# Products 512 columns wide, a token-major gated feed-forward and weights loaded in pairs: a two-layer encoder trunk on one core

## The chip, the core and the metric

The kernel runs on one core of a Trainium2 chip. TensorE (PE) multiplies, with its weight loads shown as an engine of their own (PEld); VectorE (DVE), ScalarE (ACT) and GpSimd (POOL) work element by element; SyncE (SP) issues nearly all the DMAs. PE reads SBUF and writes PSUM, whose banks here hold 128 x 512 floats. The metric is the device time of one execution in microseconds (us), as the median of several runs; lower is better.

## The reference

The input x is 256 tokens of 1024 features, in float32. Two layers, each of them:

```
x += 1/2 * (silu(n(x) @ w1) * (n(x) @ w3)) @ w2        # feed-forward 1, 1024 -> 2816 -> 1024
proj = n(x) @ w_in                                      # 1024 -> 3840 columns
A = retention(4 heads), B = HGRN2 (4 heads), C = RG-LRU # chunks of 64 tokens, from proj
x += concat(A, B, C) @ w_out
x += cross_attention(n(x), n(mem))                      # 4 heads, 256 memory tokens: wq, wkv, wo
x += 1/2 * (silu(n(x) @ w1) * (n(x) @ w3)) @ w2        # feed-forward 2
```

`n` is an RMSNorm with a gain; a last norm closes the trunk. All weights are float32, about 214 MB, and each is read once.

## The kernel before

**Products in three parts.** Every float32 operand of a large product is split into two float32r parts, hi + lo, and the product is the sum of three: hi\*hi, hi\*lo and lo\*hi (`mm3`, lines L175 to L178; the two PE lines in the profile are L169 and L171). Each of the three is one TensorE instruction with a stationary operand of 128 x 128 and a moving one of 128 x 256.

**Two ways round.** In `gemm_w` the weight piece is stationary and the 256 tokens stream, so that the result is feature-major (features on partitions). It makes w1, w3, w2, six of the fifteen 256-column pieces of w_in, the keys, w_out, wq and wo. In `gemm_x` the tokens are stationary and 256 weight columns stream, so that the result is token-major: nine pieces of w_in, the values, and the very last w2 (`final`).

**Weights.** `Weights` streams the weights in pieces of 512 rows x 256 columns (512 KB, 414 loads in all) through four raw buffers. `_split` makes the two parts: ACT copies to float32r (L82), DVE subtracts (L83). There are three buffers for the parts, so the split of a piece waits until PE is through with the piece three before it; `take` issues splits three ahead and loads five ahead.

**Feed-forward.** For every 256 of the 2816 columns, w1 and w3 give u and v for two 128-feature tiles. DVE multiplies by 1 / rms (L372, tile `R`, the factor in every row), ACT takes silu, DVE multiplies (L376), and `split` makes `g_hi` and `g_lo`. `residual` then multiplies by w2, adds to xT tile by tile (`add_tile`, L345) and makes the two parts of the next norm's input, `xn_hi` and `xn_lo`. `finish` makes `R` with a plain float32 product (L337).

**Mixers and attention.** `STEPS` sets the order in which the w_in pieces and the elementwise chains of HGRN2, retention and RG-LRU come. A scheduler then orders each engine's instructions; products that wait for nothing (the keys and the values of the cross-attention, `mem_h` and `mem_l`) fill the time in which the chains run on DVE and ACT. At the end of the chains the gated heads are transposed on PE (L544) into w_out's input, `mix_hi` and `mix_lo`. In the attention the scores of each head stand ahead of the value product of the head before.

Of the kernel before, what the change touches and what calls it, by code (L numbers as in the profile page):

```python
# [15 lines left out]
P = 128  # L16
D = 1024
# [9 lines left out]
SPLIT_AHEAD = 3  # L27
LOAD_AHEAD = 5
RAW_BUFS = 4
SPLIT_OFF = 100000  # L30
EVAC_OFF = 400
O_AHEAD = 1
KV_OFF = 100000
PART_BUFS = 3
E_BUFS = 1
# [15 lines left out]
SILU = "silu_and_others"  # silu, tanh, sin  # L51
# [4 lines left out]
class Weights:  # L56
    """Streams the packed pieces of the weights and splits them into two float32r parts."""

    def __init__(self, tc, pool, flat, pieces):
        self.tc, self.nc, self.pool = tc, tc.nc, pool  # L60
        self.flat, self.pieces = flat, pieces
        self.raw, self.parts = {}, {}
        self.n_load = self.n_split = self.n_take = self.off = 0

    def _load(self):
        i = self.n_load
        self.n_load += 1
        n = self.pieces[i].nk * CW
        t = self.pool.tile([P, 4 * CW], F32, name="w_raw", tag="w_raw", bufs=RAW_BUFS)
        self.nc.sync.dma_start(  # L70
            out=t[:, 0:n], in_=self.flat[self.off:self.off + P * n].rearrange("(p c) -> p c", p=P))
        self.off += P * n
        self.raw[i] = t.rearrange("p (k c) -> p k c", k=4)

    def _split(self):
        nc, i = self.nc, self.n_split
        self.n_split += 1
        nk = self.pieces[i].nk
        t = self.raw.pop(i)
        hi = self.pool.tile([P, 4, CW], F32R, name="w_hi", tag="w_hi", bufs=PART_BUFS)  # L80
        lo = self.pool.tile([P, 4, CW], F32R, name="w_lo", tag="w_lo", bufs=PART_BUFS)
        nc.scalar.copy(hi[:, 0:nk, :], t[:, 0:nk, :])  # L82
        nc.vector.tensor_tensor(  # L83
            out=lo[:, 0:nk, :], in0=t[:, 0:nk, :], in1=hi[:, 0:nk, :].bitcast(F32), op=ALU.subtract
        )
        self.parts[i] = (hi, lo)

    def take(self, key):
        i = self.n_take
        self.n_take += 1  # L90
        assert self.pieces[i].key == key, (self.pieces[i], key)
        with self.tc.high_priority(offset=SPLIT_OFF):
            while self.n_load < min(i + LOAD_AHEAD, len(self.pieces)):
                self._load()
            while self.n_split < min(i + SPLIT_AHEAD, len(self.pieces)):
                self._split()
        return (*self.parts.pop(i), self.pieces[i].nk)
# [5 lines left out]
IN_COLS = [1536, 1792, 2048, 2304] + [int(x) for x in STEPS if x.isdigit()]  # L103


# (column piece, first row tile) of xattn_wo: the first heads' rows of some columns fill the wait for the last heads
O_ORDER = [(c, 0) for c in range(O_AHEAD)] + [(c, 4) for c in range(O_AHEAD)]
O_ORDER += [(c, k0) for c in range(O_AHEAD, 4) for k0 in (0, 4)]

Piece = namedtuple("Piece", "key name l k0 nk c0")  # L110


def weight_pieces():
    """[nk * 128, 256] pieces of the weights in the order in which they are used"""
    out = []

    def gemm(key, name, l, nk, cs):
        for c in cs:
            for k0 in range(0, nk, 4):
                out.append(Piece(key, name, l, k0, min(4, nk - k0), c))  # L120

    for l in range(DEPTH):
        for f in ("ffn1", "ffn2"):
            if f == "ffn2":
                gemm("in", "w_in", l, KD, IN_COLS)
                gemm("kv", "xattn_wkv", l, KD, range(0, 2 * D, CW))
                gemm("out", "w_out", l, KD, range(0, D, CW))
                gemm("q", "xattn_wq", l, KD, range(0, D, CW))
                out += [Piece("o", "xattn_wo", l, k0, 4, c * CW) for c, k0 in O_ORDER]
            for c in range(0, FF, CW):  # L130
                gemm("w1", f + "_w1", l, KD, [c])
                gemm("w3", f + "_w3", l, KD, [c])
            gemm("w2", f + "_w2", l, KF, range(0, D, CW))
    # the first column's pieces in halves, for an early start
    return [out[0]._replace(nk=2, k0=k0) for k0 in range(0, KD, 2)] + out[2:]
# [9 lines left out]
def trunk(ctx: ExitStack, tc: tile.TileContext, a: dict, out: bass.AP, stop=None, dbg=None):  # L145
# [9 lines left out]
    class Bank:  # L155
        """A PSUM bank in which several sums may be open: only the first product clears the written bits"""
# [18 lines left out]
        def mm3(self, acc, lhs, rhs, begin, stop):  # L175
            (lh, ll), (rh, rl) = lhs, rhs
            self.mm(acc, lh, rh, begin, False)
            self.mm(acc, lh, rl, False, False)  # L178
            self.mm(acc, ll, rh, False, stop)

    class Act:
        """Activations that need a table: each table is loaded once for a run of them, in the order of the program"""
# [14 lines left out]
        def hold(self, i):  # L197
            """the next table waits for this instruction too"""
# [14 lines left out]
    W = Weights(tc, wp, a["weights"], weight_pieces())  # L213
# [37 lines left out]
    def split(hi, lo, src, scale=None):  # L251
        """hi + lo == src (* a column) with both parts in float32r"""
# [9 lines left out]
    def gemm_w(key, nk, x, accs):  # L262
        """acc += w[:, m]^T x for two column tiles m; accs = (bank, acc), x = (hi, lo) of [P, nk, S]"""
        xh, xl = x
        k0 = 0
        while k0 < nk:
            wh, wl, n = W.take(key)
            for m, (bank, acc) in enumerate(accs):
                for k in range(n):
                    sl = slice(m * P, (m + 1) * P)  # L270
                    bank.mm3(acc, (wh[:, k, sl], wl[:, k, sl]), (xh[:, k0 + k, :], xl[:, k0 + k, :]),
# [4 lines left out]
    def gemm_x(key, nk, x, accs, begin=True):  # L276
        """accs[t] = (bank, acc), acc += x[:, t]^T w for two token tiles t"""
        xh, xl = x
        k0 = 0
        while k0 < nk:  # L280
            wh, wl, n = W.take(key)
            for t, (bank, acc) in enumerate(accs):
                for k in range(n):
                    sl = slice(t * P, (t + 1) * P)
                    bank.mm3(acc, (xh[:, k0 + k, sl], xl[:, k0 + k, sl]), (wh[:, k, :], wl[:, k, :]),
                             begin and k0 + k == 0, k0 + k == nk - 1)
            k0 += n
            yield
# [5 lines left out]
    class Norm:  # L294
        """RMSNorm of the residual: x * g goes out in two float32r parts, the 1 / rms is applied after the product"""

        def __init__(self, l, name, mem=False):
            self.gains = col(l, name)
            if not mem:
                self.hi = keep.tile([P, KD, S], F32R, name="xn_hi", tag="xn_hi", bufs=1)  # L300
                self.lo = keep.tile([P, KD, S], F32R, name="xn_lo", tag="xn_lo", bufs=1)
            self.ssq = small.tile([P, S], F32, name="ssq", tag="ssq", bufs=2)

        def parts(self, j, xj):
            split(self.hi[:, j, :], self.lo[:, j, :], xj, self.gains[:, j:j + 1])

        def square_first(self, j, xj):
            """square() on GpSimd, for the start, when the other engines are wanted for the splits"""
            if j == 0:
                nc.gpsimd.tensor_tensor(out=self.ssq, in0=xj, in1=xj, op=ALU.mult)  # L310
            else:
                sq = small.tile([P, S], F32, name="sq", tag="sq", bufs=2)
# [3 lines left out]
        def square(self, j, xj):  # L316
            if j == 0:
                nc.scalar.square(self.ssq, xj)
            else:
                sq = small.tile([P, S], F32, name="sq", tag="sq", bufs=2)  # L320
# [3 lines left out]
        def finish(self, R=None):  # L324
            """1 / rms, rc in columns and R in every row"""
            pr = aux_bank()
            self.R = small.tile([P, S], F32, name="R", tag="R", bufs=2) if R is None else R
# [3 lines left out]
            rsqrt_col(self.rc, pr[:, 0:2], 2)  # L331
            dg = small.tile([P, 2, P], F32, name="r_diag", tag="r_diag", bufs=1)
# [7 lines left out]
        @property  # L340
        def x(self):
            return self.hi, self.lo

    def add_tile(j, acc, scale, nxt):
        nc.vector.scalar_tensor_tensor(out=xT[:, j, :], in0=acc, scalar=scale, in1=xT[:, j, :],  # L345
                                       op0=ALU.mult, op1=ALU.add)
# [3 lines left out]
    def residual(key, nk, x, scale, nxt):  # L350
        """xT += scale * (w^T x), and prepares the next norm tile by tile"""
        for c in range(0, KD, 2):
            banks = [mm_bank(2) for _ in range(2)]
            yield from gemm_w(key, nk, x, [(b, b[:, 0, :]) for b in banks])
            for m in range(2):
                add_tile(c + m, banks[m][:, 0, :], scale, nxt)
        nxt.finish()

# [1 line left out]
    def ffn(l, f, nrm, nxt, last=False, setup=None):  # L360
        with tc.tile_pool(name="ffn", bufs=2) as fp:
            gh = fp.tile([P, KF, S], F32R, name="g_hi", bufs=1)
            gl = fp.tile([P, KF, S], F32R, name="g_lo", bufs=1)
            if setup is not None:
                setup = setup(fp)
            for c in range(0, KF, 2):
                uv = [mm_bank(2) for _ in range(2)]
                for u, key in enumerate(("w1", "w3")):
                    run(gemm_w(key, KD, nrm.x, [(b, b[:, u, :]) for b in uv]))
                for m in range(2):  # L370
# [712 lines left out]
```

## Time and profile before

| | |
|---|---|
| median of 3 runs | 1274.72 us (1274.69 to 1274.8) |
| profiled execution, first to last instruction | 1272.7 us |
| PE busy | 1256.4 us, 99% |
| DVE, ACT busy | 877.4 us (69%), 682.3 us (54%) |
| DMA | 219.64 MB, mean 173 GB/s |

The runs lie 2.0 us above the span of the profiled execution, which is what lies around the first and the last instruction. Matmuls are pipelined and their ends are modelled, so PE's busy time says only that something was always under way; how fast it went is read from the distance between starts.

### The profile page before, as it was taken

What the parts mean: (1) busy time and instruction counts of PE and PEld (TensorE: products, weight loads), DVE (VectorE), ACT (ScalarE), POOL (GpSimd) and SP (SyncE); (2) the same over time, 40 slices, a digit from 0 to 9 for tenths busy, and PEclk for the clock granted to TensorE, in tenths of its full rate; (3) what the DMA queues carried; (4) which work ended last, traced back from release to release, by engine and by line L of the source; (5) the groups of instructions that cost most, each with busy time, mean ns of one, the idle gap of its engine ahead of it and who ended that gap; (6) DMA issues with size and microseconds to landing.
All of it is one profiled execution on the core that took longest, in us unless ns stands there. A gap on an engine that the chain in (4) does not pass through costs nothing.

```text
span 1272.7 us, 26847 instructions
## 1 busy us (share of the span) xinstructions
PE 1256.4 (99%) x11134; PEld 1249.8 (98%) x11134; DVE 877.4 (69%) x1456; ACT 682.3 (54%) x1149; POOL 42.6 (3%) x68
## 2 busy tenths in 40 slices
PE   7999999999999999999999999999999999999997
PEld 7999999999999999999999999999999999999997
DVE  7886656988776676665586665578877767666653
ACT  4554445656765654444464444465577656444543
POOL 5000000000100000000000000000001000000000
PEclk9999999999999999999999999999999999999999
DMA  8756566555465465665566665654545645666563
GB/s 269 211 175 184 174 185 190 157 149 150 117 182 165 115 184 183 183 182 182 183 209 202 181 184 179 187 177 154 159 121 149 183 133 165 183 183 182 168 181 100
DMA packets 61946, 219.64 MB, mean 173 GB/s; under 512 B 6912, under 2 KB 7168, under 8 KB 61568
## 3 DMA queue, kind: packets, MB, share of 16 engines
q1 hardware_dynamic: 60768, 213.55, 56.2%
q0 software_dynamic: 768, 3.86, 0.8%
q8 instruction: 87, 1.43, 0.5%
q10 hardware_dynamic: 288, 0.52, 0.1%
q14 instruction: 35, 0.29, 0.1%
HBM read 216.85 MB, written 1.05 MB: 171 GB/s over the span
## 4 chain that ended last, share of the span: by engine, by line
PE 83%; issue 15%; DVE 1%; DMA 0%; ACT 0%; POOLq 0%; POOL 0%; SPq 0%; ACTq 0%
PE mm L171 75%; PE aux L171 2%; PE aux L663 1%; PE mm L169 1%; PE aux L661 0%; PE aux L169 0%; DVE xn_lo L258 0%; PE aux L656 0%; PE aux L800 0%; PE aux L731 0%; PE aux L788 0%; DMA xT<-in_x_t_dram 0%; PE aux L337 0%; PE aux L901 0%; DVE w_lo L83 0%
## 5 line engine op out<-in xcount | busy, mean ns | idle before, releaser
L83 DVE TENSOR_TENSOR w_lo<-w_raw,w_hi 128x1024 fp32r<-128x1024 f32 (+1 forms) x414 | 498.9, 1206 | 281.3 <-ACT w_hi L82 278.6
L82 ACT CAST w_hi<-w_raw 128x1024 fp32r<-128x1024 f32 (+1 forms) x414 | 425.5, 1029 | 491.8 <-PE mm L171 371.3
L171 PE MATMUL mm<-xn_hi,w_lo 128*128 128x256 f32 x1728 | 487.6, 285 | 2.1 <-DVE w_lo L83 2.1
L171 PE MATMUL mm<-xn_lo,w_hi 128*128 128x256 f32 x1728 | 488.0, 284 | 0.0
L171 PE MATMUL mm<-xn_hi,w_hi 128*128 128x256 f32 x1620 | 457.8, 284 | 6.2 <-ACT w_hi L82 6.2
L171 PEld LDWEIGHTS mm<-xn_hi,w_lo 128*128 128x128 f32 x1728 | 330.4, 192 | 3.4 <-DVE w_lo L83 3.0
L171 PEld LDWEIGHTS mm<-xn_lo,w_hi 128*128 128x128 f32 x1728 | 331.6, 192 | 0.1
L171 PEld LDWEIGHTS mm<-xn_hi,w_hi 128*128 128x128 f32 x1620 | 311.1, 192 | 6.3 <-ACT w_hi L82 6.2
L171 PE MATMUL mm<-g_hi,w_hi 128*128 128x256 f32 x528 | 147.1, 280 | 0.0
L171 PE MATMUL mm<-g_lo,w_hi 128*128 128x256 f32 x528 | 146.1, 278 | 0.0
L171 PE MATMUL mm<-g_hi,w_lo 128*128 128x256 f32 x528 | 145.2, 281 | 0.0
L171 PEld LDWEIGHTS mm<-g_lo,w_hi 128*128 128x128 f32 x528 | 99.3, 188 | 0.0
L171 PEld LDWEIGHTS mm<-g_hi,w_hi 128*128 128x128 f32 x528 | 99.3, 188 | 0.0
L171 PEld LDWEIGHTS mm<-g_hi,w_lo 128*128 128x128 f32 x528 | 97.9, 188 | 0.0
L171 PE MATMUL mm<-w_hi,xn_lo 128*128 128x256 f32 x288 | 81.8, 284 | 0.0
L171 PE MATMUL mm<-w_lo,xn_hi 128*128 128x256 f32 x288 | 81.8, 284 | 0.0
L171 PE MATMUL mm<-w_hi,xn_hi 128*128 128x256 f32 x270 | 76.4, 285 | 0.0
L372 DVE TENSOR_TENSOR f_t<-mm,R 128x512 f32<-128x512 f32 x88 | 60.1, 687 | 3.6 <-ACT R L338 1.4
L171 PEld LDWEIGHTS mm<-w_hi,xn_lo 128*128 128x128 f32 x288 | 55.2, 192 | 0.1
L171 PEld LDWEIGHTS mm<-w_lo,xn_hi 128*128 128x128 f32 x288 | 55.2, 192 | 0.1
L171 PEld LDWEIGHTS mm<-w_hi,xn_hi 128*128 128x128 f32 x270 | 51.5, 192 | 0.0
L171 PE MATMUL mm<-w_lo,g_hi 128*128 128x256 f32 x176 | 49.3, 281 | 0.0
(269 smaller groups left out, 1955.7 us busy)
## 6 DMA issues: line engine op xcount, KB each, us to landing
w_raw<-in_weights_dram SPq DMA_DIRECT2D x394, 512.0 KB, 3.7
w_raw<-in_weights_dram SPq DMA_DIRECT2D x20, 256.0 KB, 2.7
m_t<-in_mem_t_dram POOLq DMA_DIRECT2D x2, 1024.0 KB, 7.9
xT<-in_x_t_dram SPq DMA_DIRECT2D x4, 256.0 KB, 4.9
cst<-in_c_cst_dram POOLq DMA_DIRECT2D x1, 696.0 KB, 6.4
gw<-in_gates_w_dram POOLq DMA_DIRECT2D x2, 256.0 KB, 8.5
fg<-in_final_norm_g_dram POOLq DMA_DIRECT2D x1, 512.0 KB, 5.9
out_dram<-y SPq DMA_DIRECT2D x2, 256.0 KB, 2.6
```

Source lines behind the costliest of these rows:

```text
L82: nc.scalar.copy(hi[:, 0:nk, :], t[:, 0:nk, :])
L83: nc.vector.tensor_tensor(out=lo[:, 0:nk, :], in0=t[:, 0:nk, :], in1=hi[:, 0:nk, :].bitcast(F32), op=ALU.subtract)
L169: nc.tensor.matmul(acc, lhsT, rhs, start=False, stop=stop, skip_group_check=True)
L171: i = nc.tensor.matmul(acc, lhsT, rhs, start=begin, stop=stop, skip_group_check=True)
L372: nc.vector.tensor_tensor(out=t, in0=uv[m].ap, in1=nrm.R[:, None, :].to_broadcast([P, 2, S]), op=ALU.mult)
L663: nc.tensor.matmul(sb[bs, i, :], ke[:, 1 + i, cb], qe[:, 1 + i, cb], start=True, stop=True, skip_group_check=True)
```

## The change

**Storage and widths.** The two parts of an activation now lie side by side in one tile (`xn`, `g`, `mix`, `mem_n`, each `[P, K, 2, S]`). In `gemm_w`, `mm_w` multiplies the high weight part by both activation parts at once, 512 columns into a whole PSUM bank, and the low weight part by the high activation part, 256 columns into the second half: two instructions and two weight loads where three were, and the two halves are added afterwards (`split_sum`, two additions in `add_tile`, `w_pair`). In `gemm_x` two 256-column weight pieces stream side by side, 512 columns: three instructions where six were. `gemm_x1` keeps the old form for the one unpaired piece of w_in.

**Feed-forward.** u and v are now made token-major by `gemm_x`, w1's and w3's columns side by side. `gate` applies silu with the row's 1 / rms as ACT's scale and multiplies on DVE; `turn` transposes the result on PE, four 128 x 128 tiles for every 256 columns, half a group of columns later, and splits it into `g`. `R` is made only where the mixers need it.

**Weights.** A unit is a pair of pieces; there are two raw buffers of a pair each in place of four of a piece. A unit that is used side by side is split in steps of two row tiles of both pieces.

```diff
-RAW_BUFS = 4
+RAW_BUFS = 2
...
+        u, unit, at, nk = self.steps[i]
+        while self.n_load < len(self.pieces) and self.pieces[self.n_load][0] <= u:
+            self._load()
...
+        nc.scalar.copy(hi, t)
+        nc.vector.tensor_tensor(out=lo, in0=t, in1=hi.bitcast(F32), op=ALU.subtract)
...
-STEPS = ("2560 decay0 2816 head0 decay1 3328 3584 head1 decay2 0 256 head2 decay3 512 768 rope 1024 lru head3 ret0 ret1 "
-         "1280 3072 ret2 ret3 silu ret hgrn lrutail keys").split()
+STEPS = ("2560 decay0 3328 head0 decay1 3584 3072 head1 decay2 0 head2 decay3 512 rope 1024 lru head3 ret0 ret1 "
+         "ret2 ret3 silu ret hgrn lrutail keys").split()
+W_COLS, X_COLS = (3328, 3584), (0, 512, 1024, 2560)
...
+        def mm_w(self, wh, wl, x, begin, stop):
+
+            self.mm(self.ap, wh, x, begin, stop)
+            self.mm(self.ap[:, 1, :], wl, x[:, 0, :], False, stop)
...
+    def split_sum(hi, lo, bank):
+
+        i = nc.scalar.copy(hi, bank[:, 0, :])
+        t = small.tile([P, S], F32, name="part", tag="sq", bufs=3)
+        nc.vector.tensor_tensor(out=t, in0=bank[:, 0, :], in1=hi.bitcast(F32), op=ALU.subtract)
+        nc.vector.tensor_tensor(out=lo, in0=bank[:, 1, :], in1=t, op=ALU.add)
+        return i
...
+                    bank.mm3(bank.ap, (x[:, k0 + k, 0, sl], x[:, k0 + k, 1, sl]), (wh[:, :, k, :], wl[:, :, k, :]),
                              k0 + k == 0, k0 + k == nk - 1)
...
+            if R is None and not rows:
+                return
...
+    def add_tile(j, bank, scale, nxt):
+        for u in range(2):
+            nc.vector.scalar_tensor_tensor(out=xT[:, j, :], in0=bank[:, u, :], scalar=scale, in1=xT[:, j, :],
+                                           op0=ALU.mult, op1=ALU.add)
...
+                    act(SILU, out=s, in_=banks[t][:, 0, :], func=AF.Silu, scale=r)
+                    nc.vector.scalar_tensor_tensor(out=s, in0=banks[t][:, 1, :], scalar=r, in1=s,
+                                                   op0=ALU.mult, op1=ALU.mult)
...
+                for t in range(2):
+                    for m in range(2):
+                        nc.tensor.transpose(tp[:, m, t * P:(t + 1) * P], s[t][:, m * P:(m + 1) * P], ident)
+                split(g[:, c:c + 2, 0, :], g[:, c:c + 2, 1, :], tp)
...
+                for i, _ in enumerate(gemm_x("w13", KD, nrm.x, banks)):
+                    if i == 1 and before is not None:
+                        turn(c - 2, before)
+                before = gate(banks)
...
+                for m, bank in enumerate(banks):
+                    t = small.tile([P, S], F32, name="part", tag="sq", bufs=3)
+                    nc.scalar.copy(t, bank[:, 1, :])
+                    nc.vector.tensor_tensor(out=dst[:, j + m, :], in0=bank[:, 0, :], in1=t, op=ALU.add)
+                v = dst[:, j:j + 2, :]
+                nc.vector.tensor_tensor(out=v, in0=v, in1=R[:, None, :].to_broadcast([P, 2, S]), op=ALU.mult)
```

**PE in the feed-forward.** A row names the tile written, then the moving and the stationary tile, and the moving shape. In the first feed-forward's w1 product, before:

```order
L171 MATMUL mm<-xn_hi,w_lo 128x256
L171 MATMUL mm<-xn_hi,w_hi 128x256
L171 MATMUL mm<-xn_lo,w_hi 128x256
L171 MATMUL mm<-xn_hi,w_lo 128x256
L171 MATMUL mm<-xn_hi,w_hi 128x256
L171 MATMUL mm<-xn_lo,w_hi 128x256
L171 MATMUL mm<-xn_hi,w_lo 128x256
```

In a w1 and w3 product of the changed kernel, in the middle of a group of 256 columns (`f_s` is the gated tile of the group before, `cst` the identity):

```order
L203 MATMUL mm<-w_lo,xn 128x512 x2
L203 MATMUL mm<-w_hi,xn 128x512 x2
L203 MATMUL mm<-w_lo,xn 128x512
L433 MATMUL aux<-cst,f_s 128x128 x2
L203 MATMUL mm<-w_hi,xn 128x512 x3
L203 MATMUL mm<-w_lo,xn 128x512
L203 MATMUL mm<-w_hi,xn 128x512
L433 MATMUL aux<-cst,f_s 128x128 x2
L203 MATMUL mm<-w_hi,xn 128x512
L203 MATMUL mm<-w_lo,xn 128x512
```

Weights and activations have changed places, the rows are twice as wide, and four transposes stand among the 48 products of each group.

**PE at the end of the first layer's mixers.** Before, products of the values (`mem_h`, `mem_l`) stand between the last transposes of the gated heads and up to the first product of w_out (`mix_hi`):

```order
L171 MATMUL mm<-w_hi,mem_h 128x256
L171 MATMUL mm<-w_lo,mem_h 128x256
L171 MATMUL mm<-w_hi,mem_l 128x256
L544 MATMUL aux<-cst,hg 128x128 x2
L171 MATMUL mm<-w_hi,mem_h 128x256
L171 MATMUL mm<-w_lo,mem_h 128x256
L544 MATMUL aux<-cst,hg 128x128 x2
L171 MATMUL mm<-w_hi,mem_l 128x256
L171 MATMUL mm<-w_hi,mem_h 128x256
L171 MATMUL mm<-w_lo,mem_h 128x256
L171 MATMUL mm<-w_hi,mem_l 128x256
L171 MATMUL mm<-mix_hi,w_hi 128x256
```

After, the last product of the values (`mem_n`) stands ahead of the end of the retention (`rv,rs` and `qT,kT`):

```order
L203 MATMUL mm<-w_hi,mem_n 128x512
L203 MATMUL mm<-w_lo,mem_n 128x512
L203 MATMUL aux<-rv,rs 128x96
L201 MATMUL aux<-rv,rs 128x96
L873 MATMUL aux<-qT,kT 128x256
L874 MATMUL aux<-qT,kT 128x128
L203 MATMUL aux<-rv,rs 128x96 x2
L201 MATMUL aux<-rv,rs 128x96
L203 MATMUL aux<-rv,rs 128x96
L606 MATMUL aux<-cst,rg 128x128 x3
L606 MATMUL aux<-cst,hg 128x128 x2
L606 MATMUL aux<-cst,rg 128x128 x3
```

The independent products have moved forward, ahead of the end of the chains.

**SP in the first feed-forward.** These are the weight loads with the semaphores that each waits for (`DMAHW` an earlier load's queue, `DVE` the split that frees the raw buffer). Before:

```order
L70 DMA w_raw<-in_weights_dram 128x1024 [waits DMAHW0_49,DVE_49]
L70 DMA w_raw<-in_weights_dram 128x1024 [waits DMAHW1_49,DVE_49]
L70 DMA w_raw<-in_weights_dram 128x1024 [waits DMAHW2_49,DVE_49]
L70 DMA w_raw<-in_weights_dram 128x1024 [waits DMAHW3_49,DVE_49]
L70 DMA w_raw<-in_weights_dram 128x1024 [waits DMAHW4_49,DVE_49]
```

After:

```order
L79 DMA w_raw<-in_weights_dram 128x1024 [waits DMAHW1_49,DMAHW0_49,DVE_49]
L79 DMA w_raw<-in_weights_dram 128x1024
L79 DMA w_raw<-in_weights_dram 128x1024 [waits DMAHW3_49,DMAHW2_49,DVE_49]
L79 DMA w_raw<-in_weights_dram 128x1024
L79 DMA w_raw<-in_weights_dram 128x1024 [waits DMAHW5_49,DMAHW4_49,DVE_49]
L79 DMA w_raw<-in_weights_dram 128x1024
```

Two loads now start together behind one split.

## Rows read from the trace of the kernel before

**Rows 1.** The page: span, busy time, granted clock, DMA, chain by engine.

```profile
span 1272.7 us, 26847 instructions
...
PE 1256.4 (99%) x11134; PEld 1249.8 (98%) x11134; DVE 877.4 (69%) x1456; ACT 682.3 (54%) x1149; POOL 42.6 (3%) x68
...
PEclk9999999999999999999999999999999999999999
...
GB/s 269 211 175 184 174 185 190 157 149 150 117 182 165 115 184 183 183 182 182 183 209 202 181 184 179 187 177 154 159 121 149 183 133 165 183 183 182 168 181 100
...
PE 83%; issue 15%; DVE 1%; DMA 0%; ACT 0%; POOLq 0%; POOL 0%; SPq 0%; ACTq 0%
```

**Rows 2.** The chain in order of time, runs of products: start us, us, what.

```profile
78.14 9.96 PE mm L171 x83
...
347.92 5.64 PE mm L171 x47
...
364.47 24.32 PE mm L171 x208
...
760.99 67.83 PE mm L171 x575
```

**Rows 3.** The chain from 396 to 400 us: a plain float32 product, two records.

```profile
398.22 0.43 PE aux L337 x2
```

**Rows 4.** Timeline of PEld, retention's weight loads under 96-column products: start us, us.

```profile
341.94 0.30 PEld L169 LDWEIGHTS aux<-rv,rs 128*128 128x128 f32 x2
342.16 0.30 PEld L171 LDWEIGHTS aux<-rv,rs 128*128 128x128 f32 x2
342.39 0.30 PEld L800 LDWEIGHTS aux<-qT,kT 96*128 96x128 f32 x2
```

**Rows 5.** The chain from 357 to 361 us: eight transposes of 128 x 128.

```profile
358.84 0.87 PE aux L544 x8
```

**Rows 6.** Groups by form: out<-in, shapes xcount | busy us, mean ns of one.

```profile
L83 DVE TENSOR_TENSOR w_lo<-w_raw,w_hi 128x1024 fp32r<-128x1024 f32 x394 | 483.2, 1227 | 263.1 <-ACT w_hi L82 260.4
...
L82 ACT CAST w_hi<-w_raw 128x1024 fp32r<-128x1024 f32 x394 | 413.2, 1049 | 463.7 <-PE mm L171 343.4 <-issue 107.7 <-ACT sq L321 6.8
...
L372 DVE TENSOR_TENSOR f_t<-mm,R 128x512 f32<-128x512 f32 x88 | 60.1, 687 | 3.6 <-ACT R L338 1.4 <-PE mm L171 0.5
...
L376 DVE TENSOR_TENSOR f_s<-f_s,f_t 128x256 f32<-128x256 f32 x88 | 33.8, 419 | 0.1
...
L345 DVE SCALAR_TENSOR_TENSOR xT<-mm,xT 128x256 f32<-128x256 f32 x56 | 23.0, 420 | 19.3 <-PE mm L171 19.2
...
L255 DVE TENSOR_TENSOR k_mem<-mm,k_mem 128x512 fp32r<-128x512 f32 x8 | 5.5, 684 | 0.0
...
L337 PE MATMUL aux<-r_diag,mean 128*128 128x256 f32 x18 | 5.3, 377 | 0.0
...
L788 PE MATMUL aux<-cst,ro 128*96 128x128 f32 x32 | 4.5, 272 | 0.0
```

**Rows 7.** The page, DMA issues: count, KB each, us to landing.

```profile
w_raw<-in_weights_dram SPq DMA_DIRECT2D x394, 512.0 KB, 3.7
...
m_t<-in_mem_t_dram POOLq DMA_DIRECT2D x2, 1024.0 KB, 7.9
```

**Rows 8.** Timeline of DVE, last HGRN2 head to w_out's input: start us, us.

```profile
325.29 0.36 DVE L668 TENSOR_TENSOR hm<-aux,cst 128x192 f32<-128x192 f32 x1 [3.64 <-PE aux L665]
...
355.11 1.02 DVE L843 TENSOR_TENSOR rg<-rg,or 128x384 f32<-128x384 f32 x2
...
360.63 1.66 DVE L258 SCALAR_TENSOR_TENSOR mix_lo<-aux,vec,mix_hi 128x256 fp32r<-128x256 f32 x4
```

**Rows 9.** Stretches of the first layer's mixers: busy us (x) by engine, clock, DMA.

```profile
213.00:325.00 112.00, 112.00 (x1263) 110.43 (x1262) 93.24 (x206) 72.07 (x127) 2.97 (x7) 1.00 0.51 151
325.00:364.50 39.50, 39.50 (x333) 39.25 (x331) 30.85 (x63) 27.55 (x74) 4.46 (x5) 1.00 0.52 148
```

**Rows 10.** Timeline of the start: the second weight piece, PE's first product.

```profile
6.19 0.58 PE L171 MATMUL mm<-xn_hi,w_hi 128*128 128x256 f32 x1 [6.19 <-ACT w_hi L82]
...
7.20 0.62 ACT L82 CAST w_hi<-w_raw 128x512 fp32r<-128x512 f32 x1 [0.17 <-DMA w_raw<-in_weights_dram]
```

More of the change, by code (lines that the diff above doesn't have):

```diff
@@ L56, with __init__ @@
 class Weights:
-    def __init__(self, tc, pool, flat, pieces):
+    def __init__(self, tc, pool, flat, units):
         self.tc, self.nc, self.pool = tc, tc.nc, pool
-        self.flat, self.pieces = flat, pieces
+        self.flat = flat
+        self.pieces = [(u, h, p) for u, unit in enumerate(units) for h, p in enumerate(unit.pieces)]
+        self.steps = []
+        for u, unit in enumerate(units):
+            if unit.beside:
+                nk = unit.pieces[0].nk
+                self.steps += [(u, unit, k, min(2, nk - k)) for k in range(0, nk, 2)]
+            else:
+                self.steps += [(u, unit, h, p.nk) for h, p in enumerate(unit.pieces)]
         self.raw, self.parts = {}, {}
@@ L77, in _split @@
         self.n_split += 1
[L78 to L85, printed above, removed]
+        u, unit, at, nk = self.steps[i]
+        while self.n_load < len(self.pieces) and self.pieces[self.n_load][0] <= u:
+            self._load()
+        hi = self.pool.tile([P, 4 * CW], F32R, name="w_hi", tag="w_hi", bufs=PART_BUFS)
+        lo = self.pool.tile([P, 4 * CW], F32R, name="w_lo", tag="w_lo", bufs=PART_BUFS)
+        if unit.beside:
+            hi, lo = (t.rearrange("p (h k c) -> p h k c", h=2, k=2)[:, :, 0:nk, :] for t in (hi, lo))
+            t = self.raw[u].rearrange("p h (k c) -> p h k c", k=4)[:, :, at:at + nk, :]
+        else:
+            hi, lo = (t.rearrange("p (k c) -> p k c", k=4)[:, 0:nk, :] for t in (hi, lo))
+            t = self.raw[u].rearrange("p h (k c) -> p h k c", k=4)[:, at, 0:nk, :]
+        nc.scalar.copy(hi, t)
+        nc.vector.tensor_tensor(out=lo, in0=t, in1=hi.bitcast(F32), op=ALU.subtract)
         self.parts[i] = (hi, lo)
@@ L260, in split, with gemm_w @@
         return i
-    def gemm_w(key, nk, x, accs):
-        xh, xl = x
+    def split_sum(hi, lo, bank):
[4 more added lines that the diff above has]
+        return i
+    def gemm_w(key, nk, x, banks):
         k0 = 0
@@ L347, in add_tile, with residual @@
         nxt.parts(j, xT[:, j, :])
         nxt.square(j, xT[:, j, :])
-    def residual(key, nk, x, scale, nxt):
+    def residual(key, nk, x, scale, nxt, rows=False):
         for c in range(0, KD, 2):
             banks = [mm_bank(2) for _ in range(2)]
-            yield from gemm_w(key, nk, x, [(b, b[:, 0, :]) for b in banks])
+            yield from gemm_w(key, nk, x, banks)
             for m in range(2):
-                add_tile(c + m, banks[m][:, 0, :], scale, nxt)
-        nxt.finish()
+                add_tile(c + m, banks[m], scale, nxt)
+        nxt.finish(rows=rows)
@@ L380, in ffn @@
             run(setup or ())
-            if not last:
-                run(residual("w2", KF, (gh, gl), 0.5, nxt))
-            else:
-                final((gh, gl), fp)
+            down = final(g, fp) if last else residual("w2", KF, g, 0.5, nxt, rows=f == "ffn1")
+            for i, _ in enumerate(down):
+                if i == 0:
+                    turn(KF - 2, before)
     def final(g, fp):
@@ L858, in mixer @@
                 x_cols(int(step))
-        v_mem = [values(h) for h in range(NH)]
-        run(residual("out", KD, (mh, ml), 1.0, nxt))
+        v_mem = values() + values()
+        run(residual("out", KD, mix, 1.0, nxt))
         return k_mem, v_mem
```

277 lines of the change are left out of this document (145 added, 132 removed).

## The prediction

> **What bounds the kernel now.** I read the page first. PE is busy 99% of a span of 1272.7 us, at the full clock of 2.4 GHz in every slice, and it holds 83% of the chain; DVE and ACT are far below, and the DMA rate swings between 100 and 269 GB/s without a slice in which PE pauses [rows 1]. Busy time can't say how fast PE went, so I went to the chain in order of time, where an entry is a run of back-to-back products whose length divided by their count is the distance between starts. That is .120 us in the feed-forward (9.96 / 83), .120 in the values, .117 in w_out and .118 in w2 [rows 2]. At 2.4 GHz 256 columns would stream in .107. The reader is to see that something other than the stream sets the pace, and I looked for it at the two extremes. Where it is long, a plain float32 product of 256 columns leaves two records (18 for 9 calls), each some 512 steps, and two take .43: .215 a record against .213 for 512 steps at the full clock, with the load hidden [rows 3]. Where it is short, under the retention's products of 96 columns (.040 of streaming each), two weight loads still take .225 us, so a load costs about .1125 [rows 4]. So I read the 256-wide products as paced by their weight loads. All sums below are made on the profiled span, 1272.7 us; the runs lie 2.0 us above it, and so does my forecast.
>
> **The change, part by part.** *Products.* By the loops there are 9,696 products of 256 columns now. 8,368 of them become 4,184 of 512 columns: 2,952 pairs of `gemm_x` one wide product each, 1,232 triples of `gemm_w` one wide and one narrow; 96 stay single. For a wide product I take .215. The bounds are .213 (nothing but the stream) and .240 (two times .120, no gain from a wide pair); in between lies .227, if the .013 over .107 is a cost of each instruction, whatever its width. I take the low end since the wide record of [rows 3] is the nearest thing in the trace: it has its own load and shows no such cost. A narrow product keeps its .117 to .120.
>
> - w1 and w3: 2,112 pairs x (.240 - .215) = -52.8 us.
> - w2 of three feed-forwards: 528 triples x (2 x .118 - .215) = -11.1; the last w2: 264 pairs x .021 = -5.5.
> - the mixers' pieces of w_in, keys and values: 576 pairs and 320 triples x .025 = -22.4.
> - queries: 128 triples x .025 = -3.2; w_out and wo: 256 x (2 x .117 - .215) = -4.9.
> - `R`'s rows are left out of six of the nine calls of `finish`: 6 x .43 = -2.6.
>
> Together -102.5. *Transposes* are added: 44 groups of columns x 4 = 176. Eight of the same shape took .87 us in a row, .109 each [rows 5], so +19.2. Taken singly a transpose reads 272 ns [rows 6], but that is its latency, which the next instruction does not wait for; that figure is the upper bound (+47.9) and a rival below.
>
> Beside this, the Trainium skill, "TensorE: Matmul & The Clock Gate", section "Part 4: PE-mode transpose", gives about 275 ns for a 128 x 128 transpose in a kernel and says that transposes do not bring the full clock. The mean of one agrees with the trace; the eight in .87 us and the clock, full throughout [rows 1], do not bear out that PE is held that long. By the page's figure the term would be 48 us, by the row it is 19.
>
> *Splits and gating in the feed-forward* I cost at nothing on the path. For 256 columns PE needs 48 x .215 + 4 x .109 = 10.8 us. Beside that DVE makes four w_lo (4 x 1.23), two gating products (about .5 each, between the .42 and .69 of L376 and L372) and one lo part (.69), ACT four casts (4 x 1.05), two silu and one copy (about 2): 6.6 and 6.2 us [rows 6]. The gated tile is transposed half a group later, some 5 us, against about 2 us of silu and product. Without that cover each us would be paid 44 times.
>
> *Weight supply.* Today a 512 KB load lands in 3.7 us, one 1,024 KB load in 7.9 [rows 7]. Now two of 512 KB start together behind the split that frees their buffer. Their landing lies between 3.7 and 7.9; I estimate 7.4, twice 3.7. A unit is taken apart in two steps or more of 12 products, 2.6 us each; by the order of SP and the three part buffers, a pair has about five such steps less two splits (5 x 2.65 - 2 x 2.4) = 8.4 us. So it fits, with 1 us to spare. Beyond 8.4, each us costs PE about 2/5 us for each of 207 units, 83 us in all.
>
> *The mixers' end* is the term that I think will be given back. Today the chain from the last HGRN2 head (hm, 325.29) to the end of the gated retention (rg, 355.11 + 1.02) takes 30.8 us [rows 8]; in the stretch up to w_out DVE is busy 30.85 of 39.5 us [rows 9], and PE is covered in full by 269 products of keys and values (32 us), as the built order has them. After the change that order leaves 36 wide products there, 36 x .215 = 7.7 us, with some 7 us of small products and transposes: 15 us. DVE's work in the stretch falls by four w_lo and one split, 4 x 1.23 + .69 = 5.6; with 2 to 3 us for transposing and splitting (mix_lo [rows 8]) the chain is still 28. PE waits 13 us in each layer, +26; the bounds are 0 and 26 a layer (a chain as long as today's and 3 us more, with only the 36 wide products beside it). What is late next is w_out's first product, and w_out, the attention and all behind it with it. Ahead of that stretch DVE has 93.24 of 112 us today [rows 9]; it takes on about eight more w_lo, +.83 for each of six pieces made by `w_pair` (.42 + .42 + .69 against .69) and some +1 for each key head (against k_mem's .684 [rows 6]): 113 or so in about 125 us that now belong to that work. I cost that at 0; it could reach 5 a layer.
>
> *Smaller waits.* `add_tile` now makes two additions of .42 each for a tile [rows 6]; at the end of a residual the next product waits for two tiles, +.7 in each of four places, +3. The attention's `split_sum` takes four operations of DVE and two of ACT for a head instead of one and one, +.8 a head, of which I count half: +4 (bounds 0 and 6.6). At the start the first product (6.19 today) waits for both pieces of a pair rather than one, about 2 us later, but the wait for the second piece's split [rows 10] goes: -1.5, give or take 3. The wider last columns add .5. Waits together: 26 + 3 + 4 - 1.5 + .5 = +32.
>
> Sum: -102.5 + 19.2 + 32 = -51.3, so 1221.4 of span and 1223.4 as a run; **1224 us**.
>
> **The rivals.**
> 1. *The mixers' end is hidden.* If the small products and the values are drawn out so that PE does not wait, 26 us come back: **1198**. For it: the stretch is covered to the last us today. Against it: the values' products end before the retention does in the built order, and 15 us don't cover 28.
> 2. *A cost of each instruction.* If the .013 is paid by every product, wide ones at .227 (.225 in w2 and w_out), 46 us of the gain are gone (4,184 wide products x .011): **1270**, scarcely faster. For it: .120 is above .1125 too. Against it: [rows 3].
> 3. *The stream of two parts sets the pace,* .240 a wide product, no gain on the products at all: -2.6 + 19.2 + 32 = +48.6, **1323**, slower. For it: streams of 256 columns at .117 to .120 everywhere, whichever side is stationary [rows 2]. Against it: [rows 3, 4].
> 4. *The pairs land late,* slower. If two loads together take over 8.4 us, PE waits on the splits of every unit. At 9.0 us the gain of 51 is gone (.6 x 83); at 9.4 it is **1307**. For it: a 1,024 KB load took 7.9 [rows 7], and the rate must rise as PE gets faster. Against it: 269 GB/s at the start shows that the queues can give more than the mean [rows 1].
> 5. *The transposes hold PE for their full 272 ns* [rows 6]: 47.9 in place of 19.2, **1253**. Against it: eight in .87 us [rows 5].
>
> **How the numbers follow.** The forecast has .61, its own range being 1208 to 1244 (the mixers' end between 5 and 18 us a layer, the start and attention between their bounds). Rival 1 has .10, rival 2 .13, rival 3 .05, rival 4 .07, rival 5 .04. The range 1198 to 1270 holds the forecast, rival 5, most of rival 2 and half of rival 1; outside lie rivals 3 and 4 and the rest, under .2. A measurement of this kernel tells some 0.2% (2.5 us) from no change. Faster: .61 + .10 + .04 and .09 of rival 2, .84. Same: .03, from rival 2. Slower: .05 + .07 and .01 of rival 2, .13.
>
> **What the changed profile would show.** Right: products of 512 columns .215 apart at L203 and a group of 256 columns in 10.8 us; a turn's four transposes within .5 us; pairs landing in 5.5 to 8 us, with no wait of PE for w_hi or w_lo in the feed-forward; ahead of w_out's first product about 13 us without products in each layer, with ACT, DVE and POOL on the chain there. Wrong: starts .227 or .240 apart (rivals 2 and 3), PE waiting for ACT's w_hi behind a DMA (rival 4), products less than .2 after a transpose's end but .27 after its start (rival 5), or an idle time of PE that lies elsewhere than at the mixers' end.

## The result: 1.05% slower

The changed kernel takes 1288.57 us in the median of four runs (1287.9 to 1289.2), against 1274.76 for the kernel before on the same chip: a ratio of 1.0105, 95% interval 1.009 to 1.0119. The forecast was 1224, with a range of 1198 to 1270. The page of the profiled execution shows a PE that is still the bound, but now with places where it waits. The lines answer to those of [rows 1]:

```profile
span 1286.1 us, 18728 instructions
...
PE 1240.5 (96%) x7114; PEld 1051.9 (82%) x7114; DVE 856.5 (67%) x1427; ACT 693.7 (54%) x1115; POOL 46.6 (4%) x68
...
PEclk9999999999989999999999999999999899999999
...
PE 78%; issue 14%; DVE 3%; ACT 2%; DMA 1%; POOL 0%; SPq 0%; POOLq 0%; ACTq 0%; DVEq 0%
```

PE's instructions fell by a third and its busy time by 1%: the products were merged, not saved. The two slices in which the clock shows 8 hold the mixers' ends of the two layers.

To see where the time went I took, in the timeline of PE, the start of the first product of each stage in both traces. The last column is what the forecast's terms come to for the same stage; all of the -1.5 us for the start stands in the first row.

| stage | before, us | after, us | difference | forecast |
|---|---|---|---|---|
| up to the first product | 6.2 | 8.3 | +2.1 | -1.5 |
| w1 and w3, four times | 517.1 | 507.7 | -9.4 | -35.3 |
| w2, three times | 186.6 | 185.4 | -1.2 | -11.1 |
| w_in, mixers, keys, values, two layers | 325.2 | 342.1 | +17.0 | +3.6 |
| w_out, queries, attention, wo, two layers | 166.2 | 170.4 | +4.2 | -2.0 |
| last w2 and the end | 71.5 | 72.2 | +0.7 | -5.0 |
| sum (span) | 1272.7 | 1286.1 | +13.4 | -51.3 |

**What a wide product costs.** The chain of the changed kernel in order of time (start us, us, what), in the middle of a feed-forward and in a w2:

```profile
498.95 0.22 PE aux L433 x2
499.17 9.77 PE mm L203 x43
508.93 0.22 PE aux L433 x2
509.15 1.17 PE mm L203 x5
```

```profile
589.77 10.32 PE mm L203 x59
```

A wide product takes 9.77 / 43 = .227 us, not .215; the transposes take .11 each, as [rows 5] had it. In w2 a wide and a narrow product alternate at a mean of .175, .350 for the two, where three narrow ones took .354 [rows 2]. In the last w2, token-major, 130 records of .39 us touch a stretch of 30 us, which makes a wide product (30 + .39) / 130 = .234 (columns as in [rows 9]):

```profile
1230.00:1260.00 30.00, 30.00 (x130) 24.17 (x129) 15.69 (x16) 12.21 (x15) 0.00 (x0) 1.00 0.53 176
```

A group of w1 and w3 so takes 9.77 + 2 x .22 + 1.17 = 11.4 us against 96 x .120 = 11.5 before.

**The mixers' end.** Busy time of the engines in the first layer's last 15 us ahead of w_out and in the whole stretch (columns as in [rows 9]), and then the end of the chain:

```profile
358.00:373.00 15.00, 5.35 (x28) 4.42 (x29) 9.69 (x33) 9.98 (x37) 2.75 (x4) 0.69 0.10 41
201.90:373.00 171.10, 160.50 (x1236) 138.35 (x1235) 139.58 (x309) 109.85 (x220) 12.00 (x14) 0.97 0.44 148
```

```profile
366.46 0.72 ACT or L786 x2
...
367.81 0.71 POOL st_r L286
...
369.24 0.57 DVE rg L918
...
369.86 1.34 PE aux L606 x5
371.20 0.02 issue
371.22 0.48 ACT mix L294
371.70 0.03 issue
371.73 0.49 DVE mix L295
372.22 0.04 issue
372.27 1.11 PE aux L606 x4
373.38 2.73 PE mm L203 x14
```

In the last 15 us PE works for 5.35 and the granted clock sinks to a mean of .69, which is between the full 2.4 GHz and the lower level of 1.2 GHz; the chain passes through ACT, POOL and DVE until the gated heads are transposed. The timeline of DVE, by the tiles of [rows 8], shows when that chain began:

```profile
345.38 0.36 DVE L741 TENSOR_TENSOR hm<-aux,cst 128x192 f32<-128x192 f32 x1 [3.06 <-PE aux L738]
...
369.24 1.03 DVE L918 TENSOR_TENSOR rg<-rg,or 128x384 f32<-128x384 f32 x2 [0.53 <-ACT or L786]
```

From the last hm to the end of rg it is 24.9 us, shorter than the 30.8 of [rows 8]; but the last hm itself comes 20 us later than at 325.29. The stretch before it and the one behind it:

```profile
201.93:345.38 143.45, 142.71 (x1143) 123.50 (x1141) 118.56 (x255) 89.75 (x154) 6.78 (x9) 1.00 0.48 162
345.38:373.03 27.65, 17.79 (x94) 14.86 (x95) 21.02 (x54) 20.13 (x67) 5.22 (x5) 0.83 0.22 76
```

Ahead of that hm PE is busy for all but .7 us at the full clock: it is PE's own work, in the order that the scheduler gave it, that sets the time of the hm there (which itself waits for PE), and not a late chain on DVE or ACT. Behind it 36 products of the values are left, where 269 of keys and values were before.

### The profile page after: what moved, and what is told of

Same layout as the page of the kernel before. It is cut to its first block, busy times and chain, and to the rows that moved or that the text cites. A ratio compares the mean times of both kernels' runs of the same rounds, so it can differ in the third digit from the quotient of the medians.

```text
span 1286.1 us, 18728 instructions
## 1 busy us (share of the span) xinstructions
PE 1240.5 (96%) x7114; PEld 1051.9 (82%) x7114; DVE 856.5 (67%) x1427; ACT 693.7 (54%) x1115; POOL 46.6 (4%) x68
## 3 DMA queue, kind: packets, MB, share of 16 engines
HBM read 216.85 MB, written 1.05 MB: 169 GB/s over the span
## 4 chain that ended last, share of the span: by engine, by line
PE 78%; issue 14%; DVE 3%; ACT 2%; DMA 1%; POOL 0%; SPq 0%; POOLq 0%; ACTq 0%; DVEq 0%
PE mm L203 71%; PE aux L203 2%; PE aux L736 1%; PE aux L433 1%; DMA w_raw<-in_weights_dram 1%; DVE w_lo L98 1%; ACT w_hi L97 0%; PE aux L734 0%; PE aux L606 0%; DMA xT<-in_x_t_dram 0%; DVE xn L295 0%; ACT h_sq L781 0%; ACT or L786 0%; ACT o L291 0%; PE aux L201 0%
## 5 line engine op out<-in xcount | busy, mean ns | idle before, releaser
L203 PE MATMUL mm<-w_hi,xn 128*128 128x512 f32 (+1 forms) x1726 | 525.9, 391 | 9.1 <-ACT w_hi L97 9.1
L203 PEld LDWEIGHTS mm<-w_hi,xn 128*128 128x128 f32 x1726 | 319.1, 189 | 70.5 <-ACT w_hi L97 9.5
L203 PE MATMUL mm<-w_lo,xn 128*128 128x512 f32 (+1 forms) x864 | 322.0, 388 | 1.4 <-DVE w_lo L98 1.3
L203 PEld LDWEIGHTS mm<-w_lo,xn 128*128 128x128 f32 x864 | 162.7, 188 | 35.1 <-DVE w_lo L98 3.6
L203 PE MATMUL mm<-g,w_hi 128*128 128x512 f32 x528 | 181.8, 392 | 0.0
L203 PE MATMUL mm<-g,w_lo 128*128 128x256 f32 x528 | 143.0, 282 | 0.0
L203 PEld LDWEIGHTS mm<-g,w_hi 128*128 128x128 f32 x528 | 96.9, 188 | 19.2
L203 PE MATMUL mm<-xn,w_hi 128*128 128x512 f32 x320 | 111.6, 396 | 0.0
L203 PEld LDWEIGHTS mm<-g,w_lo 128*128 128x128 f32 x528 | 99.4, 188 | 2.8
L203 PE MATMUL mm<-xn,w_lo 128*128 128x256 f32 x320 | 86.1, 281 | 0.0
```

The source lines that it names most:

```text
L203: i = nc.tensor.matmul(acc, lhsT, rhs, start=begin, stop=stop, skip_group_check=True)
```

## Experiments

On the products one theory stood against three rivals. Theory 1: each product in float32r pays its stream at 2.4 GHz and some .013 us more, at 256 columns as at 512, so that widening saves one such cost for two products and nothing of the stream. Its rivals: the stream itself sets the pace; the .012 between .227 and .215 is a wait for the PSUM bank that the product before still writes; it goes by the columns of the stationary part. On the mixers: their chains are late for the wider products and their evacuations (theory 1), or for what lies ahead of them. All ratios are to the kernel before, on the same chip.

**Each wide product as two of 256 columns** (`halves`).

```diff
-            self.mm(self.ap, wh, x, begin, stop)
+            for u in range(2):
+                self.mm(self.ap[:, u, :], wh, x[:, u, :], begin, stop)
...
-                    bank.mm3(bank.ap, (x[:, k0 + k, 0, sl], x[:, k0 + k, 1, sl]), (wh[:, :, k, :], wl[:, :, k, :]),
-                             k0 + k == 0, k0 + k == nk - 1)
+                    for u in range(2):
+                        bank.mm3(bank[:, u, :], (x[:, k0 + k, 0, sl], x[:, k0 + k, 1, sl]),
+                                 (wh[:, u, k, :], wl[:, u, k, :]), k0 + k == 0, k0 + k == nk - 1)
```

> The changed kernel with each of its 4,184 wide products made as two of 256 columns, all else left. Theory 1 (every product pays its stream at 2.4 GHz and .013 us beside it, whatever its width): starts at .120 us, 4,184 x .0133 = 55.6 us more product time; some 12 of that lie in the mixers, where PE waits anyway, so 1332 to 1344 us. Rival (the stream of the moving parts sets the pace, so that width changes nothing): 1289 us within 3.

Measured 1314.71 us, ratio 1.0311 (1.0296 to 1.0326). The chain in the feed-forward:

```profile
505.85 6.11 PE mm L203 x51
```

.120 again. The second feed-forward's w1 and w3 take 131.4 us against 125.1, and all four 24 us more: that is the gain of width on 2,112 products. The stream as the pace is out. The time lies below theory 1's 1332, which I had worked out for all 4,184 wide products: in w2 the two halves cost .29 us a pass and no more (62.09 against 61.80), as a wide product beside a narrow one hardly gains there, and the mixers got 1.5 to 2.2 us shorter, since PE waits there anyway.

**The two open banks in turns** (`banks`).

```diff
-            for t, bank in enumerate(banks):
-                for k in range(n):
...
+            for k in range(n):
+                for i, (u, w) in enumerate(((0, wh), (1, wh), (0, wl))):
+                    for t, bank in enumerate(banks):
+                        bank.mm(bank.ap, x[:, k0 + k, u, t * P:(t + 1) * P], w[:, :, k, :],
+                                k0 + k == i == 0, k0 + k == nk - 1 and i == 2)
```

(and the same in `gemm_w`.)

> The changed kernel with the products of the two open PSUM banks taken in turns, so that no product adds to the bank of the one before it. Rival to a fixed cost of each instruction: the .012 us between .227 and .215 is a wait for the bank that the product before still writes. Then starts in the feed-forward come to .215 and the time falls by 2,376 x .012 = 28 us or more, to 1261 or less. If the cost is the instruction's own: .227 as before and 1289 us within 3.

Measured 1297.2 us, ratio 1.017 (1.0153 to 1.0187). The chain:

```profile
505.41 10.91 PE mm L203 x48
```

.227 as before: the bank is not the reason. That the kernel is 9 us slower than the changed one would fit both banks of a group now being complete only at its end; this was not tested.

**Half of the stationary columns** (`st64`).

```diff
-                    sl = slice(t * P, (t + 1) * P)
-                    bank.mm3(bank.ap, ...
+                    m = 64 if W.steps[W.n_take - 1][1].pieces[0].name == "ffn2_w1" and k0 + k else P
+                    sl = slice(t * P, t * P + m)
+                    bank.mm3(bank.ap[0:m], ...
```

> The changed kernel with 64 columns of the stationary part in place of 128 in 7 of 8 row tiles of w1 and w3 of both second feed-forwards (it leaves out half of the tokens there). If the .0133 us beside the stream is for loading 128 columns and goes by their number, starts there come to .220 us (or .215 if a load of 64 is hidden in full), and the time falls by 924 x .0067 = 6 us; if it is a cost of the instruction, .227 and 1289 us.

One run: 1291.23 us. The chain, and PEld's group of these loads (busy us, mean ns):

```profile
500.65 9.89 PE mm L203 x43
```

```profile
L203 PEld LDWEIGHTS mm<-w_hi,xn 128*64 128x64 f32 x616 | 82.3, 134 | 50.9
```

The load's record is shorter (134 ns against 189), the products' starts are .230 apart: no gain at 512 columns. At 256 it was not tried.

**The parts in bfloat16, in the changed kernel and in the kernel before** (`bf16`, `before_bf16`). The parts then hold fewer bits than those of float32r; order and number of instructions are almost the same.

```diff
-F32R = mybir.dt.float32r
+F32R = mybir.dt.bfloat16
...
-        nc.vector.tensor_tensor(out=lo, in0=t, in1=hi.bitcast(F32), op=ALU.subtract)
+        nc.vector.tensor_tensor(out=lo, in0=t, in1=hi, op=ALU.subtract)
```

> The changed kernel with all high and low parts in bfloat16 in place of float32r (a product with fewer bits; the number of instructions stays). If the .0133 us beside the stream belongs to float32r's four-byte parts, starts of wide products fall to about .215 us, and the time by some 35 us, to 1255 or less. If every product pays it whatever its type, .227 us, and the time changes only by what the shorter splits give the mixers' end, 1270 to 1289 us.

> The kernel before with its high and low parts in bfloat16 (a product with fewer bits), 256 columns wide throughout. Theory 1 (the .0133 us beside the stream is float32r's own and not the weight load's): starts fall from .120 to about .109 us, 9,696 products x .011 = 107 us less of PE work; in the mixers the chains of DVE and ACT will not keep up, so 1180 to 1215 us, and the width of a product would gain nothing there. Rival (weight loads pace products of 256 columns, as the forecast read it): starts stay at .1125 us or more, the wide products' .216 keep an advantage, and the time is 1205 us or more.

One run each: 1224.01 us for the changed kernel and 1180.23 for the kernel before. Their chains, the changed one first, and a group of PEld of the second:

```profile
508.81 9.28 PE mm L203 x43
```

```profile
507.24 9.06 PE mm L171 x83
```

```profile
L171 PEld LDWEIGHTS <-w_hi 128*128 128x128 bf16 x5156 | 505.5, 98 | 66.9 <-ACT w_hi L82 6.3 <-issue 1.0
```

.216 for 512 columns and .109 for 256: some .0025 beside the stream at either width, where float32r pays .0133. So the cost goes with float32r, and with it gone the narrow kernel is 44 us faster than the wide one, which still carries the transposes and the mixers' wait. The same page of the Trainium skill that the prediction names, "TensorE: Matmul & The Clock Gate", section "Wait — 56ns, not 53.3ns?", gives N / 2.4 GHz plus about 2.5 ns for products back to back, 215.7 ns for 512 columns; the bfloat16 rows agree, and the float32r rows (.120 and .227) do not. The weight loads change with the type too (98 ns a record here, 189 in float32r), so this swap does not tell whether the load or the product pays.

**The mixers, part by part.** Four kernels put parts of the changed one back: `w_pair` to three narrow products with one evacuation; the token-major pieces of w_in and their order; both, with keys and values; and that with narrow products and one addition in w2 and w_out as well.

```diff
-            banks = [mm_bank(2) for _ in range(2)]
-            yield from gemm_w("in", KD, nrm.x, banks)
+            bank = mm_bank(2)
+            gemm_w3("in", nrm.x, bank)
             with tc.high_priority(offset=EVAC_OFF):
-                for m, bank in enumerate(banks):
...
+                nc.vector.tensor_tensor(out=dst[:, j:j + 2, :], in0=bank.ap,
+                                        in1=R[:, None, :].to_broadcast([P, 2, S]), op=ALU.mult)
...
-X_COLS = (0, 512, 1024, 2560)
+X_COLS = ()
...
-        for u in range(2):
+        for u in range(1 if narrow else 2):
             nc.vector.scalar_tensor_tensor(out=xT[:, j, :], in0=bank[:, u, :], scalar=scale, in1=xT[:, j, :],
```

> The changed kernel with the six w_pair pieces of w_in alone as before the change: three products of 256 columns, one evacuation of .69 us on DVE in place of two copies on ACT, two additions and one product on DVE. Theory 1a (these longer evacuations make the decays and the last HGRN2 head late): the mixers' stretch goes from 171 to 166 or 167 us, 1279 to 1281 us in all, near the 1278 of the run with all of the mixers narrow. Theory 1b (the order: a 512-column piece stands ahead of the first head and makes all heads late): 170 to 172 us, 1288 to 1291 us.

> The changed kernel with the token-major pieces of w_in alone 256 columns wide and in the order of before the change; w_pair, keys and values stay as changed. Theory 1b (order): the mixers' stretch goes from 171 to 167 us or less, 1281 us or less in all. Theory 1a (evacuations): 169 us or more, 1285 us or more.

> The changed kernel with the mixers' products, their order and their evacuations as before the change (w_in, keys and values 256 columns wide). Theory 1 (the wider products and their evacuations make the chains of DVE and ACT late, and PE waits some 14 us a layer at their end): the stretch from the first product of w_in to the first of w_out goes from 171 back to 163 us in each layer, 1272 us in all. Rival (the chains are late for what lies ahead of the mixers: two additions in add_tile, R made 2 us later, splits of pairs): the stretch stays above 168 us, and PE's products are 6 us a layer longer: 1283 to 1290 us.

> The changed kernel with the mixers' products as before the change and those of w2 and w_out too (one addition in add_tile in place of two). If the 2.7 us a layer that the mixers' stretch stayed longer (165.5 against 162.8) come from the second additions, which make R late, it comes back to 163 us, and the time to 1271 to 1274 us. If they come from the way weights are split in pairs: 165 us and 1277 to 1280 us.

| kernel | median, us | ratio (interval) | mixers' stretch, layers 1 and 2 |
|---|---|---|---|
| changed | 1288.57 | 1.0105 (1.009 to 1.0119) | 171.1, 171.0 |
| w_pair narrow | 1284.07 | 1.0066 (1.0051 to 1.0081) | 167.3, 168.0 |
| w_in pieces and order of before | 1284.24 | 1.0069 (1.0052 to 1.0086) | 168.8, 168.8 |
| all of the mixers narrow | 1278.02 | 1.0022 (1.0012 to 1.0031) | 165.5, 165.9 |
| and w2 and w_out narrow | 1275.55 | .9999 (.999 to 1.0009) | 162.4, 164.3 |
| before | 1274.8 to 1275.6 | | 162.8, 162.4 |

All four came out between the times that their theories gave. Neither 1a nor 1b had it alone: of the 8.5 us that the stretch grew, `w_pair` gives back 3.4 and the order 2.3, together (with keys and values) 5.4, and the residual's products and second additions another 1.6 to 3.1. But each of these kernels has another order of PE's products as well. In the first layer the products of keys and values that are left behind the last hm are 36 wide ones in the changed kernel, 60 with `w_pair` narrow and 80 with the order of before, and 236 narrow ones with all of the mixers narrow, 248 with w2 and w_out too and 269 before: every kernel with a shorter stretch than the changed one has more of them there. So the four kernels do not separate a longer evacuation from the cover that an order leaves. With all of the mixers narrow the stretch has this busy time in the first layer:

```profile
203.60:369.10 165.50, 163.11 (x1684) 160.86 (x1683) 132.25 (x284) 106.65 (x210) 9.59 (x14) 1.00 0.42 154
```

PE is busy for all but 2.4 us, and no longer at a lower clock (1.00).

**Only w1 and w3 changed** (`ffn_wide`, `ffn_wide2`, `ffn_both`). The first two take the kernel before with the token-major w1 and w3 alone, each step one load of 512 KB; the third keeps them feature-major, in pairs of a wide and a narrow product:

```diff
...
+                for k in range(n):
+                    sl, xk = slice(m * P, (m + 1) * P), x[:, k0 + k]
+                    bank.mm(bank.ap, wh[:, k, sl], xk, k0 + k == 0, False)
+                    bank.mm(bank[:, 1, :], wl[:, k, sl], xk[:, 0, :], False, k0 + k == KD - 1)
...
```

> The kernel before with the feed-forward's w1 and w3 alone changed: token-major, 512 columns wide, transposed behind, each step's weights one 512 KB load of two row tiles of both matrices; mixers, attention, w2 and the four raw buffers as before. By the stage times (127.6 against 125.1 us for w1 and w3) 4 x 2.45 = 10 us are gained, and the rest stays: 1263 to 1267 us. Rival (what the changed kernel lost in the mixers comes from the feed-forward ahead of them, such as R made late): the mixers' stretch is over 165 us again, and the time 1270 us or more.

> The kernel of the run before last with a change of w1 and w3 alone (512 columns, token-major), and the memory's elementwise work one group of columns later, so that DVE does not wait in line for the memory's DMA ahead of w_lo (9.5 us in the second layer's first feed-forward). If that wait was what kept it from the 1263 to 1267 us: 1265 to 1268 us. If not: 1271 us.

> The kernel before with w1 and w3 left feature-major, but w_hi times both activation parts in one product of 512 columns (and w_lo times the high part in one of 256); no transposes. A pair takes .347 us where w2 was measured, against .360 before and .355 with the token-major form's transposes: 32 pairs a group, 44 groups: 1,408 x .013 = 18 us gained, 1255 to 1260 us. Rival (the two halves of each sum cost DVE 1.7 us a tile more work beside w_lo, and PE waits for its four PSUM banks): 1270 us or more.

Measured 1271.05 us (ratio .9961, .9946 to .9975), 1271.2 (.9966, .9953 to .9979) and 1266.52 (.9929, .9909 to .9949). In the first the mixers' stretch is 162.8 and 162.4 us, as in the kernel before: the feed-forward is not what made them late, though the time is the one that the rival gave. The chain of its second layer's first feed-forward stands behind the memory's DMA:

```profile
644.18 9.48 DMA m_t<-in_mem_t_dram
...
654.02 2.43 DVE m_t L533 x7
...
659.97 1.15 DVE w_lo L83
661.11 0.04 issue
661.16 5.78 PE mm L170 x24
```

In the second kernel the edit (one more `yield` ahead of `setup_mem`) moved nothing: DVE's work on the memory, at 654.02 us in the first, still begins at 653.9, and w1 and w3 there take 128.9 us, after 129.1 in the first and 125.2 in the changed kernel. So it tells nothing of what the wait costs, and that stays open. The third is the fastest kernel in float32r here, without transposes; w1 and w3 take 124.9 to 132.9 us, and of the 18 us expected half came, since a wide and a narrow product take .353 there (2 x 95.07 / 539), not .347: 1,408 x .007 = 10 us. The chain in the second feed-forward, and the page, which shows PE busy for 99% and DVE at 75%:

```profile
474.98 95.07 PE mm L171 x539
```

```profile
PE 1246.0 (99%) x9726; PEld 1172.3 (93%) x9726; DVE 949.5 (75%) x1720; ACT 736.0 (58%) x1325; POOL 42.6 (3%) x68
```

## Why the prediction was wrong

**The step that failed is the price of a wide product.** "For a wide product I take .215 ... since the wide record of [rows 3] is the nearest thing in the trace: it has its own load and shows no such cost." That record is a plain float32 product; the kernel's wide products are float32r, and those take .227. The reading ahead of it, that weight loads at .1125 pace the 256-wide products [rows 4], is not borne out: at 512 columns, where a load of .1125 would be hidden, the same .0133 stands beside the stream, and halving the loaded columns there gains nothing. What was wanted was in [rows 2]: .120 less .107 there is the same .013, the "cost of each instruction" of rival 2, which I held for unlikely at .13. With rival 2's prices (.227, and .225 in w2 and w_out) the same terms come to a span of 1269.5 us in place of 1221.4: the mis-sized term is 48 of the 65 us between forecast and result. In w2 it takes most of what a wide product could bring: the pair measured .350 where .333 was forecast and three narrow ones take .354.

**The other 17 us,** by the table's stages at those prices: w2 4.6 and the last w2 and the end 3.1, the start 3.6, the mixers 2.7, w_out to wo 2.1, w1 and w3 .6. Most of the first two is the same step again, as rival 2's .225 is too low there: a pair in w2 measured .350 and not .343, 528 x .007 = 3.7, and a wide product in the last w2 .234, 264 x .009 = 2.4. At the start the first product came 2.1 us later, as forecast (after [rows 10], 6.19), but nothing was won behind it: the first pass of w1 and w3 took 6.7 us more than the second (131.8 against 125.1), where it had been 6.0. The chain stands on two weight loads there, which the prediction's weight supply had in time:

```profile
8.33 1.65 PE L203 MATMUL mm<-w_hi,xn 128*128 128x512 f32 x3 [8.33 <-ACT w_hi L97]
```

```profile
16.95 5.75 DMA w_raw<-in_weights_dram
...
26.64 7.77 DMA w_raw<-in_weights_dram
```

**What was right.** The mixers' end: the products there gained 576 x .013 + 320 x .013 = 11.7 us and the stretches grew by 17.0, so PE's wait is some 28.7 us, 14.3 a layer, where 13 was forecast; 10.6 of the 14.3 show as idle time (171.10 less 160.50). ACT, DVE and POOL stand on the chain there. The mechanism held too: from the last hm to w_out it is 27.65 us, where the forecast had 28, with the 36 wide products that it counted. That the hm comes 20 us later is nearly all in its terms: 13 us from the order (125 us of work ahead where there were 112) and 896 x .012 / 2 = 5.4 from the price of wide products. The DVE work ahead, costed at 0, cost PE nothing there, as PE waited .7 us ahead of the hm. The transposes at .109 held, against rival 5 (.22 for two). The pairs land in time once the kernel runs, and sooner than the 5.5 to 8 us forecast (rival 4 is out): the page has

```profile
w_raw<-in_weights_dram SPq DMA_DIRECT2D x392, 512.0 KB, 4.3
```

The splits and gating cost PE nothing: three of the four w1 and w3 stages took 125.1 to 125.7 us, 11 groups of 11.4.

## What to carry to other kernels

Price an instruction by rows of its own data type: a row of another type, even with the same number of steps, can lack a cost that yours has. When the trace has one width only, ask whether the excess over the stream belongs to the instruction; then merging two products saves one excess at most (here .013 of .240 us, 5%, in w1 and w3, but only .004 of .354 in w2), and additions, transposes and waits that the merge brings have to be cheaper than that. Products that wait for nothing hide the end of a chain only for as long as they last: made shorter and moved ahead of that end, they left PE waiting for 14 us a layer, though PE, DVE and ACT are all below 100% on average.

## What the runs showed of the hardware

In w1 and w3 a float32r product with its own weight load starts .120 us after the one before at 256 columns and .227 at 512, some .0135 over the stream in both; a bfloat16 product .109 and .216, some .0025 over it. Neither the PSUM bank (.227) nor the number of stationary columns (.230) lowers the .227. The float32r cost is not the same everywhere: three narrow products in w2 take .354 and not .360, a wide and a narrow one .350 to .353 and not .347, a wide one in the last w2 .234. What it goes by, and whether it is paid in the load or in the product itself, was not separated. At the mixers' end PE was idle from 360 to 363 us at the full clock; from 364 to 373 the clock was at its lower level, .50 or 1.2 GHz, with PE busy for 2.89 of the 9 us; in the first 3 us of w_out's products it came back (columns as in [rows 9]):

```profile
360.00:363.00 3.00, 0.00 (x0) 0.00 (x0) 3.00 (x7) 2.00 (x9) 0.00 (x0) 1.00 0.00 0
364.00:373.00 9.00, 2.89 (x13) 2.20 (x13) 3.69 (x13) 5.90 (x23) 2.44 (x3) 0.50 0.00 0
373.00:376.00 3.00, 3.00 (x17) 2.65 (x16) 1.30 (x3) 0.89 (x2) 0.00 (x0) 0.86 0.00 0
376.00:385.00 9.00, 9.00 (x53) 7.94 (x53) 5.90 (x10) 4.71 (x8) 0.00 (x0) 1.00 0.35 117
```
